# Scaled copies and masks of a delta net moved from VectorE to ScalarE and GpSimd, with new planner figures and a table of chosen moves

## The chip, the cores and the metric

The kernel runs on one core of one Trainium2 chip. A core has five engines, each with its own queue that is worked in order: TensorE (PE, matrix products, results in PSUM), VectorE (DVE), ScalarE (ACT), GpSimd (POOL) and SyncE (SP, which here issues all DMAs). Engines wait for each other through semaphores. The metric is the time on the device in microseconds, lower is better.

## The reference

One step of a two-layer decoder for a prompt of 512 tokens and a sample group of 8 x 8 tokens that share all weights; all arrays are float32, the model width is 1024. Layer 0 mixes tokens by pooling, layer 1 by a gated delta net; each mixer is followed by a SwiGLU block of width 2816, and every block sits between two RMS norms. What the change touches is the delta net, 16 value heads of 128 on 8 key heads of 128. Cut to its core, for one chunk of tokens:

```python
decay = exp(where(causal, gc[i] - gc[j], -inf))       # gc: running sum of the log gates
t_mat = eye + strict(kb @ k.T * decay)                # kb = k * beta
u = solve(t_mat, v * beta); w = solve(t_mat, kb * exp(gc))
qk = q @ k.T * decay
q_dec = q * exp(gc); k_dec = k * exp(gc_last - gc)
# over the chunks, in order:
v_new = u - w @ S
o = q_dec @ S + qk @ v_new
S = S * exp(gc_last) + k_dec.T @ v_new
```

Before it, q, k and v come from one projection of 6176 columns, a causal convolution over four tokens and SiLU, and q and k are normalised by head. After it, o is normalised by head, gated by SiLU(z) and projected back.

## The kernel before

**Tiling and stages.** Activations lie transposed, 128 channels on the partitions by 576 tokens (512 + 64). To keep float32 accuracy at the fast matmul rate every operand is split in a high and a low part: `Weights.split` (line 767) makes `wh` with a copy on ACT and `wl` = raw - wh on DVE, `mm3` (line 775) issues three matmuls for each pair of tiles. The trace shows these stages, in order of time: pooling mixer and its norms, the first SwiGLU block (`ffn`, with `Strassen` for its larger part, to about 440 us), the delta net with its projections (about 500 to 1070 us), the output projection with its norms, the second SwiGLU block, and the last norm.

**The delta net** runs in four groups (`GRP`) of two key heads and four value heads. `project(G)` (line 1316) makes q, k, v of a group: 8 weight tiles of 128 columns, matmuls into the PSUM banks `ps_m`, copies `u` on ACT, the convolution `ac` as three fused instructions on DVE, transposes into `ps_x`, and from there `vt` (prompt) and `vs` (samples), scaled by `nk`, both on DVE. `core(G)` (line 1680) then works in spans of 128 tokens (`SPANS` = 4; the chunk of the reference is 64, the result does not depend on it). It loads the running gate sums as rows, adds the mask `bar` (0 or -1e30) on DVE or POOL, and takes four exponentials on ACT: this is `QD`, the decay. With it `Uw` (the strict part of t_mat) and QD (qk) are made from `ps_k`. `inv32` (line 1209) inverts blocks of 32 on DVE (tiles `ia`, `ii`), a few products put them together. `scan` (line 1611) is the recurrence: for each span and key head `pk` = products with the state S, `rs` (DVE), `t1` = gcq x pk (DVE), `pv` = Uw x rs, `vn` = bet x pv (DVE), `ve` = kde x vn (DVE or POOL), the new state from kt x ve, the output from QD x vn, then scaled by `rq` on DVE. `sample_heads` (line 1541) does the same for the 8 sample sequences, with `ve` split again in `vH` and `vL`. bet, kde, gcq, ngc, rq and nk are small tables with one number for each token and head.

**What sets the order.** No order is written out. Between `plan.start()` and `plan.finish()` the class `Plan` only records the operations with what they read and write. An operation that may run on either of two engines is recorded through `EITHER` (DVE or POOL). `finish` (line 272) then plans the whole kernel as a list: `cost` (line 160) gives each operation a duration by engine, kind and width, `forward` (line 428) puts the ready operation of best rank on each engine, with latencies between engines (`LAT`), a clock model of PE, and idle matmuls (`ps_w`, of `ones`) that it sets into PSUM banks not in use while PE would stand still for long; `backward` finds the latest start of each operation in the plan found, which gives the ranks for the next round. First come 40 rounds with random changes of the ranks, then 16 passes of `refined`: windows of 60 us in steps of 30 us, in each up to 40 random trials, the best one kept. The order so found is issued, so each engine's queue is fixed, and the engines' real semaphores do the rest. All recorded instructions have one line in the profile, L319, the line in `finish` that issues them; they are told apart by the tiles' names (L315 is an idle matmul).

Of the kernel before, what the change touches and what calls it, by code (L numbers as in the profile page):

```python
# [20 lines left out]
P = 128  # L21
# [20 lines left out]
VH = 16  # L42
# [14 lines left out]
class Plan:  # L57
# [8 lines left out]

    LAT = {"PE": 55.0, "ACT": 36.0, "DVE": 36.0, "POOL": 70.0, "SP": 60.0}
# [8 lines left out]
    PASSES, SPAN, STEP, TRIES, FEW = 16, 60000.0, 30000.0, 40, 6  # L76
# [83 lines left out]
    def cost(self, eng, method, out, ins, k):  # L160
# [24 lines left out]
        if eng == "POOL":  # L185
            if method in ("memset", "tensor_copy"):
                t = 0.85 * n + (100 if method == "memset" else 183)
            elif method == "affine_select":
                t = 1.1 * n + 190
            else:  # L190
                bc = any(list(x.ap)[-1][0] == 0 for x in ins if self.size(x) > 1)
                t = (1.75 if bc else 2.2) * n + 180
            return t - 60, t
# [3 lines left out]
        elif method == "scalar_tensor_tensor":  # L197
            t = 1.04 * n + 210
# [8 lines left out]
    def put(self, method, calls, a, k):  # L207
# [39 lines left out]
        if "PE" in calls:  # L247
# [3 lines left out]
            work *= rows * min(1.0, 0.25 * -(-cols // 32)) / 128  # L251
        elif method == "activation":
            mode = self.TABLE.get(str(a[2]).split(".")[-1], 0)
        cost = {e: self.cost(e, method, outs[0], ins, k) for e in calls}
        two = method in ("tensor_tensor", "scalar_tensor_tensor", "tensor_scalar", "tensor_copy") \
            and not any(x.space == PSUM for x in ins)
        self.ops.append((calls, cost, a, k, sorted(preds), mode, work, next(iter(calls)), two, method,
                         {x.tensor.name for x in ins + outs if x.space == PSUM}))
# [13 lines left out]
    def finish(self):  # L272
# [35 lines left out]
        for _ in range(self.PASSES):  # L308
            found = self.refined(best, draw)
            if found[0] < best[0]:  # L310
                best = found
# [9 lines left out]
    def refined(self, plan, draw):  # L321

        late = self.backward(plan[1], plan[2])
        rank = [-t for t in late]
        order = sorted(range(len(late)), key=late.__getitem__)
        names = [self.name(o) for o in self.ops]
        done, state, a, first = ([], []), None, 0.0, 0

        def behind(found, b):

            nonlocal first
            log, times, taken, busy = found[-2], found[-1], found[2], 0.0
            worst = max((t - late[i] for (i, e), (t, _) in zip(log, times) if e is not None), default=-1e12)
            while first < len(order) and state is not None and state[2][order[first]]:
                first += 1
            k = first
            while k < len(order) and taken[order[k]]:
                k += 1
            return worst if k == len(order) else max(worst, b - late[order[k]])

        while True:
            b = a + self.SPAN
            best = None
            tries = self.TRIES
            k = 0
            while k < tries:
                trial = rank
                if k:
                    off, by = {}, draw.choice(self.STIR[2:])
                    trial = rank[:]  # L350
                    for i in window:
                        off.setdefault(names[i], by * (2.0 * draw.random() - 1.0))
                        trial[i] += off[names[i]]
                found = self.forward(trial, state, b, late, best and best[0])
                k += 1
                if found is None:
                    continue
                value = behind(found, b)
                if k == 1:
                    window = [i for i, e in found[-2] if e is not None]  # L360
                    work = sum(self.ops[i][1]["PE"][0] for i, e in found[-2] if e == "PE")
                    if work > 0.995 * self.SPAN:
                        tries = self.FEW
                if best is None or value < best[0]:
                    best = value, trial
            rank = best[1]
            found = self.forward(rank, state, a + self.STEP)
            done[0].extend(found[-2])
            done[1].extend(found[-1])
            state, a = found[:-2], a + self.STEP  # L370
            if not found[0]:
                return max(found[3].values()), *done

# [54 lines left out]
    def forward(self, rank, state=None, until=None, due=None, limit=None):  # L428
# [4 lines left out]
        if state is None:  # L433
# [13 lines left out]
            quiet = {}  # L447
        else:
            todo, left, taken, free, ready, avail, when, mode, dma, port, phases, fast, recent, busy, turn, still, \
                quiet = state  # L450
            left, taken, when, recent = left[:], taken[:], when[:], recent.copy()
            free, mode, port, turn, still, quiet = (dict(v) for v in (free, mode, port, turn, still, quiet))
# [54 lines left out]
        while todo:  # L507
# [40 lines left out]
            if limit is not None and t - due[i] >= limit:  # L548
                return None
            if mine is not q:  # L550
                q.remove((-rank[i], i))
                heapq.heapify(q)
# [7 lines left out]
            if e == "PE":  # L560
                note(t, ops[i][6])
                done += hold * (fast - 1)
                hold *= fast
            taken[i] = True
# [17 lines left out]
            for j in succ[i]:  # L582
                to = ops[j][7]
                at = t + hold if to == e == "PE" else end + self.LAT[to]
# [5 lines left out]
        if until is None:  # L590
            return max(free.values()), order, times
        return (todo, left, taken, free, ready, avail, when, mode, dma, port, phases, fast, recent, busy, turn, still,
                quiet, order, times)

    def take(self, e, q, taken, mode):

        while taken[q[0][1]]:
            heapq.heappop(q)
        best = q[0]
        if self.ops[best[1]][5] not in (0, mode) and self.HOLD.get(e):  # L600
            same = min((x for x in q if not taken[x[1]] and self.ops[x[1]][5] in (0, mode)), default=None)
            if same is not None and same[0] - best[0] < self.HOLD[e]:
                best = same
        q.remove(best)
# [1408 lines left out]
```

## Time and profile before

| | |
|---|---|
| time, median of 3 runs | 1575.35 us (1569.87 to 1575.95) |
| profiled execution, its own time | 1574.86 us |
| its span, first to last instruction | 1573.1 us |
| instructions | 30432 |
| busy: PE, weight loads | 1535.2 us (98%), 1471.2 us (94%) |
| busy: DVE, ACT, POOL | 1192.2 us (76%), 788.5 us (50%), 127.0 us (8%) |
| granted PE clock | 0.996 |
| DMA | 197.86 MB, mean 126 GB/s |

PE's matmuls are pipelined, so that the record of one runs on into the next; a gap shorter than that does not show as idle time. A row of a group of instructions reads: line, engine, operation, what it writes <- what it reads, shape, count, busy time and mean of one in ns, and the idle time of the engine just before them with what ended it. A row of waits reads: who waited <- for whom, us in total, times, the longest.

### The profile page before, as it was taken

The numbers are of one execution on the slowest core, as the hardware profiler recorded it, in microseconds if no ns is written. First come the engines' busy times: TensorE is split into PE (matmuls) and PEld (weight loads), VectorE is DVE, ScalarE is ACT, GpSimd is POOL, SyncE is SP. The second block draws the span as 40 slices with busy tenths as digits, with TensorE's granted clock in tenths as the row PEclk, the third lists the DMA queues.
The fourth block names the chain that finished last, engine by engine and source line by source line (L and its number), as shares of the span: only waits on it lengthen the run. The fifth ranks groups of instructions, "written<-read, shape, count | busy, mean of one in ns | idle before, by whom it ended". The sixth has DMA issues, their size and how long they took to land. (4 is left out here: it accounts for less than half of the span.)

```text
span 1573.1 us, 30432 instructions
## 1 busy us (share of the span) xinstructions
PE 1535.2 (98%) x11931; PEld 1471.2 (94%) x11931; DVE 1192.2 (76%) x2377; ACT 788.5 (50%) x1655; POOL 127.0 (8%) x257
## 2 busy tenths in 40 slices
PE   8999999999999999999999999999999999999997
PEld 8999999999999988898899889899999999999997
DVE  6894566677686898897998899668797485766855
ACT  7663443435556955453563553425465453434553
POOL 4110000000010021100220121000020000000000
PEclk9999999999999999999999999999999999999999
DMA  6464323232566332425243433655864432233253
GB/s 184 134 181 124 103 71 112 61 107 80 168 179 171 110 102 79 141 69 143 83 132 93 126 109 100 204 160 172 244 196 136 144 93 83 76 100 108 76 169 105
DMA packets 344902, 197.86 MB, mean 126 GB/s; under 512 B 13547, under 2 KB 337740, under 8 KB 344751
## 3 DMA queue, kind: packets, MB, share of 16 engines
q1 hardware_dynamic: 344759, 195.92, 43.0%
q8 instruction: 94, 1.54, 0.4%
q14 instruction: 49, 0.40, 0.1%
HBM read 165.60 MB, written 30.52 MB: 125 GB/s over the span
## 5 line engine op out<-in xcount | busy, mean ns | idle before, releaser
L319 ACT ACTIVATE wh<-wraw 128x1024 fp32r<-128x1024 f32 (+4 forms) x240 | 232.7, 975 | 215.0 <-PE ps_A L319 74.3
L319 DVE TENSOR_TENSOR wl<-wraw,wh 128x1024 fp32r<-128x1024 f32 (+4 forms) x232 | 257.3, 1115 | 66.5 <-ACT wh L319 49.4
L319 PE MATMUL ps_m<-hH,wh 128*128 128x256 f32 (+1 forms) x832 | 248.8, 311 | 2.1 <-ACT zz L319 1.5
L319 PE MATMUL ps_m<-hL,wh 128*128 128x256 f32 (+1 forms) x832 | 248.0, 309 | 0.0
L319 PE MATMUL ps_m<-hH,wl 128*128 128x320 f32 (+1 forms) x832 | 243.4, 307 | 0.0
L319 PEld LDWEIGHTS ps_m<-hH,wh 128*128 128x128 f32 x832 | 154.8, 189 | 7.4 <-ACT zz L319 2.7
L319 PEld LDWEIGHTS ps_m<-hL,wh 128*128 128x128 f32 x832 | 155.1, 189 | 3.2 <-issue 1.7
L319 PEld LDWEIGHTS ps_m<-hH,wl 128*128 128x128 f32 x832 | 153.7, 189 | 2.5 <-issue 0.8
L319 PE MATMUL ps_B<-hH,wh 128*128 128x320 f32 (+1 forms) x444 | 129.8, 305 | 0.2 <-DVE yo L319 0.2
L319 PE MATMUL ps_B<-hL,wh 128*128 128x320 f32 (+1 forms) x444 | 128.6, 304 | 0.0
L319 PE MATMUL ps_B<-hH,wl 128*128 128x320 f32 (+1 forms) x444 | 128.6, 304 | 0.0
L319 PE MATMUL ps_A<-hH,wh 128*128 128x256 f32 (+1 forms) x432 | 118.7, 290 | 0.5 <-DVE yo L319 0.5
L319 PE MATMUL ps_A<-hL,wh 128*128 128x256 f32 (+1 forms) x432 | 118.7, 292 | 0.1
L319 PE MATMUL ps_A<-hH,wl 128*128 128x256 f32 (+1 forms) x432 | 118.2, 292 | 0.0
L319 PE MATMUL ps_A<-aH,wh 128*128 128x288 f32 x352 | 99.3, 297 | 1.4 <-ACT wh L319 1.4
L319 PE MATMUL ps_A<-aL,wh 128*128 128x288 f32 x352 | 100.0, 295 | 0.0
L319 PE MATMUL ps_A<-aH,wl 128*128 128x288 f32 x352 | 99.7, 297 | 0.0
L319 PE MATMUL ps_B<-aH,wh 128*128 128x288 f32 x352 | 98.9, 297 | 0.5 <-DVE xa L319 0.5
L319 PE MATMUL ps_B<-aL,wh 128*128 128x288 f32 x352 | 98.6, 297 | 0.0
L319 PE MATMUL ps_B<-aH,wl 128*128 128x288 f32 x352 | 96.6, 296 | 0.0
L319 PEld LDWEIGHTS ps_B<-hH,wh 128*128 128x128 f32 x444 | 82.1, 188 | 1.0 <-issue 0.5
L319 PEld LDWEIGHTS ps_B<-hH,wl 128*128 128x128 f32 x444 | 81.9, 188 | 0.3 <-DVE wl L319 0.2
(467 smaller groups left out, 4063.8 us busy)
## 6 DMA issues: line engine op xcount, KB each, us to landing
wraw<-in_ffn_w_in_dram SPq DMA_DIRECT2D x77, 512.0 KB
wraw<-in_gdn_w_in_dram SPq DMA_DIRECT2D x56, 512.0 KB
graw<-in_ffn_w_in_dram SPq DMA_DIRECT2D x33, 512.0 KB
wraw<-in_ffn_w_out_dram SPq DMA_DIRECT2D x32, 448.0 KB
wraw<-in_gdn_w_out_dram SPq DMA_DIRECT2D x24, 512.0 KB
wraw<-in_ffn_w_out_dram SPq DMA_DIRECT2D x32, 320.0 KB
St<-in_state_gdn_rec_dram SPq DMA_DIRECT2D x32, 256.0 KB
out_dram<-St SPq DMA_DIRECT2D x32, 256.0 KB
```

Of the source, the lines that this page charges most:

```text
L319: calls[e](*a, **k)
```

## The change

- **Planner.** A result that ACT hands to ACT itself arrives 88 ns later (`SAME`). On DVE and ACT an instruction that starts at another base partition than 0, or follows one, starts 32 ns after the end of the one before (`REBASE`, with a new last field in each recorded operation). Three durations change: POOL copies of more than two dimensions, narrow fused instructions on DVE, `tensor_scalar` from PSUM. Durations are rounded to an eighth of a ns. The 16 passes of random trials are replaced by 5 passes over a fixed table, `CHOSEN`: for each window of 30 us a list of seeds, each of which moves the ranks of the window's operations by a hash of the seed and the number of the tile's name (`moved`).
- **Scaled copies.** `vs`, both `t1`, the first span's output `vv`, and `ve` are made by ACT with a scale of one number per partition, one instruction for each 128 columns. `ve` no longer reads vn: it comes straight from PSUM with the scale `bk` = bet x kde, a new small table that DVE fills for each key head. In `sample_heads` `vH` comes straight from PSUM the same way, and `vL` as one fused DVE instruction per 128 columns.
- **Masks.** The 16 additions of `bar` become `affine_select` on POOL that writes -1e30 outside the triangle; `bar` itself is gone.

The diff, without the numbers of the table and without the removed body of `refined`:

```diff
+    SAME = {"ACT": 88.0}
+    REBASE = 32.0
...
-    PASSES, SPAN, STEP, TRIES, FEW = 16, 60000.0, 30000.0, 40, 6
+    SPAN, STEP = 60000.0, 30000.0
+    CHOSEN = (
...
     )
...
         if eng == "POOL":
-            if method in ("memset", "tensor_copy"):
+            if method == "tensor_copy" and len(list(out.ap)) > 2:
+                t = 5.5 * n + 250
+            elif method in ("memset", "tensor_copy"):
                 t = 0.85 * n + (100 if method == "memset" else 183)
             elif method == "affine_select":
...
         elif method == "scalar_tensor_tensor":
-            t = 1.04 * n + 210
+            t = 1.04 * n + (210 if ps or n > 64 else 152)
+        elif method == "tensor_scalar" and ps:
+            t = 1.09 * n + 200
...
-            work *= rows * min(1.0, 0.25 * -(-cols // 32)) / 128
+            work = round(8 * work * rows * min(1.0, 0.25 * -(-cols // 32)) / 128) / 8
...
-        cost = {e: self.cost(e, method, outs[0], ins, k) for e in calls}
+        cost = {e: tuple(round(8 * t) / 8 for t in self.cost(e, method, outs[0], ins, k)) for e in calls}
...
+        base = any(x.space != DRAM and x.offset >= list(x.ap)[0][0] for x in ins + outs)
         self.ops.append((calls, cost, a, k, sorted(preds), mode, work, next(iter(calls)), two, method,
-                         {x.tensor.name for x in ins + outs if x.space == PSUM}))
+                         {x.tensor.name for x in ins + outs if x.space == PSUM}, base))
 
...
-        for _ in range(self.PASSES):
-            found = self.refined(best, draw)
-            if found[0] < best[0]:
-                best = found
+        numbers = {}
+        self.number = [numbers.setdefault(self.name(o), len(numbers)) for o in ops]
+        for chosen in self.CHOSEN:
+            best = self.refined(best, chosen)
...
+    def refined(self, plan, chosen):
+
+        rank = [-t for t in self.backward(plan[1], plan[2])]
+        done, state, a = ([], []), None, 0.0
+        chosen = {int(w): [int(x) for x in seeds.split()] for w, seeds in (p.split(":") for p in chosen.split(";"))}
         while True:
...
+            seeds = chosen.get(round(a / self.STEP), ())
+            if seeds:
+                window = [i for i, e in self.forward(rank, state, a + self.SPAN)[-2] if e is not None]
+                for seed in seeds:
+                    self.moved(rank, window, seed)
+            a += self.STEP
...
+    def moved(self, rank, window, seed):
+
+        by, part, low = (300.0, 1000.0, 3000.0)[seed % 3], (1, 4, 16)[seed // 3 % 3], 0xffffffff
+        off = {}
+        for i in window:
+            k = self.number[i]
+            if k not in off:
+                y = k * 0x9e3779b1 + seed * 0xc2b2ae35 & low
+                y = (y ^ y >> 13) * 0x27d4eb2f & low
+                x = seed * 0x9e3779b1 + k * 0x85ebca6b & low
+                x = (x ^ x >> 15) * 0x2c1b3c6d & low
+                x = (x ^ x >> 12) * 0x297a2d39 & low
+                off[k] = 0.0 if (y ^ y >> 15) % part else by * (2.0 * ((x ^ x >> 15) / 4294967296.0) - 1.0)
+            rank[i] += off[k]
...
+            elif e in past:
+                if past[e][1] or ops[i][11]:
+                    late = max(past[e][0] + self.REBASE - t, 0.0)
+                    hold, done = hold + late, done + late
+                past[e] = t + done, ops[i][11]
...
-                at = t + hold if to == e == "PE" else end + self.LAT[to]
+                at = t + hold if to == e == "PE" else end + self.LAT[to] + (self.SAME.get(e, 0.0) if to == e else 0.0)
...
+    bk = sp.tile([P, SP1, VH], F32, name="bk")
...
-        bar = cst.tile([P, P], F32, name="bar")
-        DVE.tensor_scalar(bar, t_gt, -1e30, None, op0=mult)
...
+                            DVE.tensor_tensor(bk[:, :, h2], bet[:, :, h2], kde[:, :, h2], op=mult)
...
-                    DVE.tensor_scalar(vs[:SMP, i], pv, nk[:SMP, SPANS, kh:kh + 1], None, op0=mult)
+                    ACT.activation(vs[:SMP, i], pv, AF.Copy, scale=nk[:SMP, SPANS, kh:kh + 1])
...
-                rs, t1, vn, ve = sn[lo, 0], sn[up, 1], sn[:, 2], sn[:, 3]
+                rs, t1, vn = sn[lo, 0], sn[up, 1], sn[:, 2]
...
-                DVE.tensor_tensor(t1, pk[up, 0].rearrange("p (e v) -> p e v", e=2),
-                                  gcq[up, SPANS, h2].unsqueeze(2).to_broadcast([SMP, 2, P]), op=mult)
+                for e in range(2):
+                    ACT.activation(t1[:, e], pk[up, 0, e * P:(e + 1) * P], AF.Copy,
+                                   scale=gcq[up, SPANS, 2 * kh + e:2 * kh + e + 1])
...
-                EITHER.tensor_tensor(ve, vn, kde[:, SPANS, h2].unsqueeze(2).to_broadcast([P, 2, P]), op=mult)
                 vH = cp_.tile([P, 2, P], F32R, name="vH", tag="vH", bufs=1)
                 vL = cp_.tile([P, 2, P], F32R, name="vL", tag="vL", bufs=1)
-                split2(ve, vH, vL)
+                for e in range(2):
+                    by = bk[:, SPANS, 2 * kh + e:2 * kh + e + 1]
+                    ve = pv[:, 0, e * P:(e + 1) * P]
+                    ACT.activation(vH[:, e], ve, AF.Copy, scale=by)
+                    DVE.scalar_tensor_tensor(out=vL[:, e], in0=ve, scalar=by, in1=vH[:, e].bitcast(F32),
+                                             op0=mult, op1=sub)
                 yield 0.6
...
-                        DVE.tensor_tensor(t1, pk[:, 1].rearrange("p (e v) -> p e v", e=2),
-                                          gcq[:, s, hh].unsqueeze(2).to_broadcast([P, 2, P]), op=mult)
+                        for e in range(2):
+                            ACT.activation(t1[:, e], pk[:, 1, e * P:(e + 1) * P], AF.Copy,
+                                           scale=gcq[:, s, hh.start + e:hh.start + e + 1])
...
-                    EITHER.tensor_tensor(ve, vn, kde[:, s, hh].unsqueeze(2).to_broadcast([P, 2, P]), op=mult)
+                    for e in range(2):
+                        ACT.activation(ve[:, e], pv[:, 0, e * P:(e + 1) * P], AF.Copy,
+                                       scale=bk[:, s, hh.start + e:hh.start + e + 1])
...
-                        DVE.tensor_scalar(vv, pov, rqc, None, op0=mult)
+                        ACT.activation(vv, pov, AF.Copy, scale=rqc)
...
-                EITHER.tensor_tensor(de, de, bar.unsqueeze(1).to_broadcast([P, 4, P]), op=add)
+                POOL.affine_select(de, de, [[0, 4], [1, P]], ALU.is_ge, -1e30, base=0, channel_multiplier=-1)
```

More of the change, by code (lines that the diff above doesn't have):

```diff
@@ L75 @@
     ROUNDS, STIR, SEED = 40, (0.0, 0.0, 300.0, 1000.0, 3000.0), 2
-    PASSES, SPAN, STEP, TRIES, FEW = 16, 60000.0, 30000.0, 40, 6
+    SPAN, STEP = 60000.0, 30000.0
+    CHOSEN = (
[125 rows of a table added]
+    )
     def __init__(self, tc):
@@ L319, in finish @@
                 calls[e](*a, **k)
[L321 to L339, printed above, removed]
-        while True:
[L342 to L367, printed above, removed]
@@ new lines, in refined @@
+    def refined(self, plan, chosen):
+        rank = [-t for t in self.backward(plan[1], plan[2])]
+        done, state, a = ([], []), None, 0.0
+        chosen = {int(w): [int(x) for x in seeds.split()] for w, seeds in (p.split(":") for p in chosen.split(";"))}
+        while True:
+            seeds = chosen.get(round(a / self.STEP), ())
[4 more added lines that the diff above has]
+            a += self.STEP
+            found = self.forward(rank, state, a)
@@ L368, in refined @@
             done[0].extend(found[-2])
             done[1].extend(found[-1])
-            state, a = found[:-2], a + self.STEP
+            state = found[:-2]
             if not found[0]:
                 return max(found[3].values()), *done
+    def moved(self, rank, window, seed):
[11 more added lines that the diff above has]
+            rank[i] += off[k]
@@ L426, in backward, with forward @@
         return late
-    def forward(self, rank, state=None, until=None, due=None, limit=None):
+    def forward(self, rank, state=None, until=None):
         ops, succ = self.ops, self.succ
@@ L447, in forward @@
             quiet = {}
+            past = {"DVE": (0.0, False), "ACT": (0.0, False)}
         else:
             todo, left, taken, free, ready, avail, when, mode, dma, port, phases, fast, recent, busy, turn, still, \
-                quiet = state
+                quiet, past = state
             left, taken, when, recent = left[:], taken[:], when[:], recent.copy()
-            free, mode, port, turn, still, quiet = (dict(v) for v in (free, mode, port, turn, still, quiet))
+            free, mode, port, turn, still, quiet, past = (dict(v) for v in (free, mode, port, turn, still, quiet, past))
             ready = {e: v[:] for e, v in ready.items()}
@@ L547, in forward @@
             i = self.take(e, mine, taken, mode.get(e))
[L548 to L552, printed above, removed]
+            q.remove((-rank[i], i))
+            heapq.heapify(q)
             hold, done = ops[i][1][e]
@@ L592, in forward @@
         return (todo, left, taken, free, ready, avail, when, mode, dma, port, phases, fast, recent, busy, turn, still,
-                quiet, order, times)
+                quiet, past, order, times)
     def take(self, e, q, taken, mode):
-        while taken[q[0][1]]:
-            heapq.heappop(q)
-        best = q[0]
+        q = [x for x in q if not taken[x[1]]]
+        best = min(q)
         if self.ops[best[1]][5] not in (0, mode) and self.HOLD.get(e):
-            same = min((x for x in q if not taken[x[1]] and self.ops[x[1]][5] in (0, mode)), default=None)
+            same = min((x for x in q if self.ops[x[1]][5] in (0, mode)), default=None)
             if same is not None and same[0] - best[0] < self.HOLD[e]:
                 best = same
-        q.remove(best)
-        heapq.heapify(q)
         return best[1]
@@ L750, in masks @@
         DVE.scalar_tensor_tensor(out=eye2, in0=eyo, scalar=par, in1=eye2, op0=mult, op1=add)
-        return t_gt, bar, s_le2, s_gt2, s_gt_r, s_in, s_st, eye2
+        return t_gt, s_le2, s_gt2, s_gt_r, s_in, s_st, eye2
     def dup(ap):
@@ L1199, in finish0 @@
                 pre_norm(tp, back[0], acc2, hf, G_MPRE + NC)
-            t_gt, bar, s_le2, s_gt2, s_gt_r, s_in, s_st, eye2 = masks(tp)
+            t_gt, s_le2, s_gt2, s_gt_r, s_in, s_st, eye2 = masks(tp)
             s_le = s_le2[:, :SMP]
```

125 rows, old and new, of the table CHOSEN are left out of this document.

## The prediction

> **What bounds the kernel now.** I read the page first, then the busy time of each engine by stage, then who TensorE (PE) waits for in the stage that stands out, then single instructions there.
>
> ```profile
> span 1573.1 us, 30432 instructions
> ```
>
> The busy times by stage; columns: stretch, its length, then PE, weight loads, VectorE (DVE), ScalarE (ACT), GpSimd (POOL), each in us with its instructions, granted clock, DMA.
>
> ```profile
> 0.00:40.00 40.00, 35.21 (x235) 32.78 (x236) 28.07 (x74) 29.29 (x70) 18.05 (x77) 0.91 0.67 181
> 40.00:540.00 500.00, 499.12 (x3717) 490.51 (x3716) 359.97 (x642) 263.32 (x472) 22.20 (x31) 1.00 0.43 125
> 540.00:1000.00 460.00, 441.21 (x3740) 401.28 (x3738) 412.87 (x1001) 230.51 (x639) 72.21 (x134) 1.00 0.38 109
> 1000.00:1100.00 100.00, 98.40 (x795) 91.25 (x796) 68.05 (x135) 40.84 (x110) 1.25 (x1) 1.00 0.59 175
> 1100.00:1540.00 440.00, 435.90 (x3266) 431.80 (x3265) 307.89 (x504) 211.56 (x341) 13.30 (x14) 1.00 0.45 132
> 1540.00:1573.00 33.00, 25.34 (x187) 23.60 (x186) 15.31 (x27) 12.96 (x26) 0.00 (x0) 0.95 0.25 79
> ```
>
> PE is the bound everywhere: it is without work 37.8 us of the span, and half of that, 460 - 441.2 = 18.8 us, lies between 540 and 1000 us, where the four groups of the delta net run. There DVE is busy 412.87 of 460, 89.8%; in the other long stretches it has a quarter free. So DVE is the second bound of this stage and of no other. Part of PE's busy time is filler besides (matmuls of ones that keep the clock up while nothing is ready); the same stretches for the tile ps_w alone:
>
> ```profile
> 40.00:540.00 500.00, 2.03 (x10) 1.65 (x10) 1.00 0.43 125
> 540.00:1000.00 460.00, 5.92 (x40) 5.22 (x40) 1.00 0.38 109
> 1000.00:1100.00 100.00, 1.05 (x8) 0.98 (x8) 1.00 0.59 175
> 1100.00:1540.00 440.00, 2.89 (x20) 2.55 (x20) 1.00 0.45 132
> ```
>
> PE's waits between 540 and 1000 us (us in total, times, longest), the rows in which it waits for DVE:
>
> ```profile
> PE ps_x L319 <- DVE vt L319: 3.0, 4, 1.4
> PE ps_x L319 <- DVE vs L319: 2.4, 4, 0.9
> PE ps_k L319 <- DVE TQ L319: 2.0, 2, 1.1
> PE ps_k L319 <- DVE QD L319: 1.8, 3, 1.0
> PE ps_k L319 <- DVE Uw L319: 1.3, 4, 0.7
> PE ps_k L319 <- DVE T L319: 0.7, 2, 0.4
> ```
>
> They sum to 11.2 us of the 18.8, 60%. One of them, instruction by instruction:
>
> ```profile
> 704.04 0.31 PE L319 MATMUL ps_m<-hH,wh 128*128 128x320 f32 x1
> 704.19 0.31 PE L319 MATMUL ps_m<-hL,wh 128*128 128x320 f32 x1
> 704.45 0.31 PE L319 MATMUL ps_m<-hH,wl 128*128 128x320 f32 x1
> 705.09 0.34 DVE L319 TENSOR_SCALAR vs<-ps_x,nk 64x128 f32<-64x128 f32 x1
> 705.57 0.41 PE L319 MATMUL ps_x<-ident,ac 128*128 128x128 f32 x2 [0.81 <-DVE vs L319]
> ```
>
> Undisturbed, matmuls of this width start 0.15 apart (704.04, 704.19). From 704.45 to 705.57 it is 1.12: 0.97 is lost, while 0.81 is shown as idle, because a matmul's record runs on past the start of its successor. About 0.16 us is thus hidden in each stall. What PE waits for is a bank that the DVE copy vs has to empty.
>
> **The change part by part.** It has two halves: what the engines must do, and the order. PE's real matmuls, the DMAs and SP's queue keep their number.
>
> *Off DVE, onto ACT and POOL.* The operations that go, and below them the nearest rows for what comes:
>
> ```profile
> L319 DVE TENSOR_TENSOR QD<-QD,bar 128x512 f32<-128x512 f32 x16 | 10.9, 682 | 2.3 <-DMA QD<-gc_d 2.3
> L319 DVE TENSOR_SCALAR vs<-ps_x,nk 64x128 f32<-64x128 f32 x16 | 5.4, 338 | 0.2
> L319 DVE TENSOR_TENSOR t<-ps_k,gcq 128x256 f32<-128x256 f32 x24 | 9.9, 414 | 0.0
> L319 DVE TENSOR_TENSOR ve<-vn,kde 128x256 f32<-128x256 f32 x28 | 11.5, 419 | 0.2
> L319 DVE TENSOR_SCALAR vt<-ps_s,rq 128x256 f32<-128x256 f32 x8 | 3.7, 478 | 4.0 <-PE ps_s L319 4.0
> L319 DVE TENSOR_TENSOR sn<-ps_k,gcq 64x256 f32<-64x256 f32 x8 | 3.4, 428 | 0.2
> L319 DVE TENSOR_TENSOR sn<-sn,kde 128x256 f32<-128x256 f32 x6 | 2.9, 485 | 0.0
> L319 DVE TENSOR_TENSOR vL<-sn,vH 128x256 fp32r<-128x256 f32 x6 | 2.5, 422 | 0.9 <-ACT vH L319 0.9
> ...
> L319 DVE SCALAR_TENSOR_TENSOR Uw<-ps_k,bet,QD 128x128 f32<-128x128 f32 x64 | 18.9, 342 | 1.3 <-PE ps_k L319 1.1 <-issue 0.2
> L319 ACT ACTIVATE S<-ps_s 128x128 f32<-128x128 f32 x16 | 3.5, 273 | 7.0 <-PE ps_s L319 7.0
> L319 ACT ACTIVATE u<-ps_m 128x256 f32<-128x256 f32 x56 | 20.9, 378 | 25.0 <-PE ps_m L319 23.5 <-PE ps_x L319 1.2
> L319 ACT ACTIVATE y<-ps_A,prm 128x256 f32<-128x256 f32 x8 | 3.6, 470 | 0.7 <-PE ps_A L319 0.7
> L319 POOL TENSOR_SCALAR_AFFINE_SELECT eyo<-eyo 128x512 f32<-128x512 f32 x1 | 0.9, 869 | 0.1
> L319 POOL COPY u<-cstt 128x24 f32<-128x24 f32 x18 | 8.9, 503 | 26.6 <-ACT u L319 9.6 <-issue 7.9 <-ACT cstt L319 6.2
> ```
>
> DVE loses 10.9 + 5.4 + 9.9 + 11.5 + 3.7 + 3.4 + 2.9 + 2.5 = 50.2 us. It gains 16 fused instructions that make vL from PSUM, 16 x 0.342 = 5.5, and eight tiny products for bk, at most 8 x 0.342 = 2.7 and by their 10 columns nearer half, 1.3. Not all lies in the tight stage, as the instructions on ve between 540 and 1000 us show:
>
> ```profile
> 540.00:1000.00 460.00, 14.23 (x48) 7.79 (x48) 8.12 (x20) 4.00 (x4) 1.00 0.38 109
> ```
>
> 24 of 32 (4 of them on POOL): the last of four groups scans after 1000 us. So three quarters of the last six removed rows count, 25.4 of 33.9; of the masks, four a group with the first group's ahead of the stage, 8.2; all of vs, which belongs to the projections, 5.4. In the stage that is 39.0 off and 0.75 x 5.5 + 1.3 = 5.4 on. The planner now gives a POOL copy of three dimensions 5.5 ns an element instead of 0.85, so some of these go to DVE: between none and 18 at the 0.338 of the wider vs copy, 6.1; I take 4, the upper half, since the trace has them dear on POOL (503 ns). Net in the stage: 30 us, DVE from 412.9 to 383.
>
> ACT gets 160 scaled copies of 128 columns: 16 vs, 16 t1 and 16 vH of the samples, 48 t1 and 64 ve of the scan. The plain copy of that width takes 273 ns; a per-partition scale adds 470 - 378 = 92; 365 each, 58.4, and eight of 256 columns at 470, 3.8: 62.2 in all, less the eight vH copies it did before. In the stage some 46, so ACT goes from 230.5 to 277 of 460. That lies in ACT's free time; without it the price is that of the third rival. POOL gets 16 masks of 0.87, 13.9 us, in the stage 10.4 on 72.2, less the few kde products it did. Each mask stands ahead of four exponentials on ACT, at the least the 273 of a plain copy each, 1.1 us, so POOL at 0.87 keeps in front; if it didn't, those exponentials would be late next.
>
> A rule that speaks against the masks stands in the Trainium skill, "SBUF — State Buffer", section "SBUF: two separate sides": VectorE with two SBUF inputs and GpSimd take one shared port pair by an exclusive lock, the later one blocked for the whole instruction. A row with two SBUF inputs (ns min/median/max):
>
> ```profile
> L319 DVE SCALAR_TENSOR_TENSOR ac<-u,cwt,ac x96: 825/836/1452, 513.6 to 977.6; 128x600 f32<-128x600 f32 x96
> ```
>
> The longest took 616 ns more than the median and the median 11 more than the shortest, so in this row blocking is the exception. If by that rule every mask blocked VectorE, 10.4 of the 30 us would be given back, the stage's gain below would fall from 18 to 12, and the time would be 1557.
>
> *What PE gets of it.* The stage offers idle 18.8, filler 5.9, and hidden tails: 19 waits in the rows above at 0.16 are 3.0, and as many again for those of other engines would be 6; I take 5.3. Together 30. The lower end is none of it; the upper end comes from the other side: with DVE at 383 and the same 89.8% of the stage, the stage is 426 long, 34 less. I take the part in which DVE was the releaser, 60%: **18 us**.
>
> *The order.* The planner's new figures (an ACT result read by ACT 88 ns later, 32 ns where the base partition differs, dearer POOL copies) and a table of 5 passes of chosen moves replace a search inside the kernel. No row prices this. Outside the stage and between 40 and 1540 us PE has idle 0.9 + 1.6 + 4.1 and filler 2.0 + 1.1 + 2.9, together 12.5; a better order could take all, a worse one lose as much. I take half as gain, **6 us**, since one figure moves towards the trace: for the POOL copy of 24 columns and 503 ns the old one gives 0.85 x 24 + 183 = 203, the new 5.5 x 24 + 250 = 382. The 4.8 idle of the first 40 us and the 7.7 of the last 33 are chains that the change leaves alone.
>
> Sum: 1574.86 (the profiled execution; 1.8 of it outside the span) - 18 - 6 = 1550.9. The median of the runs is 0.5 higher; I say **1551**.
>
> **The rivals.**
> *DVE was worth more.* The stage shrinks with DVE (34) and most of the 12.5 outside goes (8): 1574.9 - 42 = 1533. For it: an engine at 89.8% that works in a fixed order is late for much that shows as no idle time of PE, in gaps under 0.16 us. Against: only 30 us of loss can be seen.
> *PE doesn't care.* The freed time is hidden behind matmuls anyway, the waits move to ACT: 1570 to 1577, say 1573. For it: no wait in the rows above is over 1.4 us. Against: the 704 us rows, where the moved copy itself held PE.
> *ACT in the recurrence (slower).* ve, vH and t1 now queue on ACT in order, behind the weight copies.
>
> ```profile
> L319 ACT ACTIVATE wh<-wraw 128x1024 fp32r<-128x1024 f32 x159 | 167.5, 1057 | 115.6 <-PE ps_m L319 53.2 <-PE ps_A L319 24.5 <-PE ps_B L319 24.5
> ```
>
> Before, a step had vn then ve on DVE, 0.42 + 0.42; now two copies of 0.365 straight from PSUM, 0.73, plus up to 1.06 behind a weight copy: +0.95. There are 16 serial steps and 8 sample heads: 24 x 0.95 = 23; at ACT's 60% busy, 14 us: 1589 if nothing is gained elsewhere. Behind them on ACT stand the next wh copies, and for those wait wl on DVE and the projection's matmuls. It decides once ACT is so full that the plan can't set the scaled copies ahead of wh; against it, ACT sat idle 115.6 us ahead of its wh copies. The Trainium skill, "ScalarE: Activation LUTs", section "Rules for kernel authors", says the same in general: multiplications belong on VectorE, not ScalarE. The rows agree per element (365 ns for 128 columns against 414 for 256), and 62 us of ACT for 50 of DVE is the price of its breach.
> *The table doesn't fit.* Its numbers mean something only for the list of operations they were chosen on. If it was another list, ranks are moved at random by up to 3 us, and each of the 23 slices of the stage may look like the worst one:
>
> ```profile
> 980.00:1000.00 20.00, 17.51 (x228) 16.19 (x226) 16.95 (x35) 10.54 (x23) 3.29 (x4) 1.00 0.57 175
> ```
>
> 23 x 2.49 = 57 idle instead of 18.8, +38, against the 24 gained: 1589. Against it: the table is densest in its windows 15 to 35 of 30 us, 450 to 1080, where the trace has the delta net.
>
> **How the numbers follow.** Forecast 0.50, more from DVE 0.24, no effect 0.13, ACT in the recurrence 0.08, table unfit 0.05. A measurement tells 0.5%, 8 us, from no change: the first two are faster (0.74), the third is the same (0.13), the last two slower (0.13). The range leaves out the slower cases and the far end of the second: 1530 (all 12.5 outside and the 34: 1528) to 1576; the forecast's own is 1541 (34 gained) to 1562 (12).
>
> **What would show it.** Right: between 540 us and the end of the third group's projection PE idle falls from 18.8 to under 10, DVE busy by about 30 (over the span by 50.2 - 6.8 - 4 = 39), ACT's rises by some 60 over the span, the wait of ps_x for DVE vs is gone, and the stages before and after keep their lengths. Wrong: DVE falls and PE's idle time stays (second rival), PE waits for ACT ve or vH (third), or PE idles and filler grows in the weight-streaming stages too (fourth). A gain that lies outside 540 to 1100 us would be the order's, not the engines'.

## The result, and the profile after

The changed kernel takes 1553.05 us (median of 4 runs, 1552.07 to 1555.61) against 1573.22 us (4 runs, 1569.87 to 1575.95): 0.9875 of the time before, interval 0.9848 to 0.9902. The forecast was 1551. The number holds; the runs below show that its reason does not.

The head of the page after:

```profile
span 1550.3 us, 30447 instructions
...
PE 1519.0 (98%) x11875; PEld 1456.1 (94%) x11875; DVE 1162.7 (75%) x2292; ACT 831.7 (54%) x1809; POOL 130.1 (8%) x261
```

DVE lost 29.5 us, ACT took on 43.2, POOL 3.1. The busy times by stage after (stretch, its length, then PE, weight loads, DVE, ACT, POOL with their instructions, clock, DMA):

```profile
40.00:540.00 500.00, 497.98 (x3730) 489.28 (x3730) 365.19 (x664) 267.14 (x485) 23.55 (x38) 1.00 0.44 125
540.00:1000.00 460.00, 447.29 (x3875) 409.43 (x3877) 393.19 (x925) 269.36 (x777) 78.38 (x135) 1.00 0.42 118
1000.00:1100.00 100.00, 96.86 (x748) 89.44 (x739) 66.71 (x125) 48.05 (x129) 0.24 (x1) 1.00 0.63 181
1100.00:1540.00 440.00, 438.11 (x3293) 434.19 (x3292) 307.33 (x507) 215.89 (x349) 11.16 (x12) 1.00 0.43 124
```

The filler (tile ps_w) after, in the same stretches:

```profile
40.00:540.00 500.00, 1.95 (x10) 1.53 (x10) 1.00 0.44 125
540.00:1000.00 460.00, 0.39 (x2) 0.30 (x2) 1.00 0.42 118
1000.00:1100.00 100.00, 0.00 (x0) 0.00 (x0) 1.00 0.63 181
1100.00:1540.00 440.00, 2.28 (x16) 2.02 (x16) 1.00 0.43 124
```

In the stage PE idle fell from 18.8 to 12.7 us and filler from 5.9 to 0.4. Over the span there are 11817 real matmuls in both kernels (all of PE's less the filler's 114 before, 58 after), so the 22.8 us of span split into three: idle 37.9 to 31.3, filler 18.6 to 10.6, and the records of the real matmuls 1516.6 to 1508.4. The last part, 8.2 us, is at least in part time that stalls hide behind a record's tail; the granted clock can have a share, since it was 0.91 in the first 40 us before and 1.00 there after, which is up to 3.6 us.

Who PE waits for after, between 540 and 1000 us:

```profile
PE ps_x L453 <- DVE vt L453: 3.8, 4, 1.8
PE ps_k L453 <- DVE QD L453: 1.4, 2, 0.9
PE ps_s L453 <- DVE sn L453: 1.2, 4, 0.4
PE ps_s L453 <- DVE vs L453: 1.2, 3, 0.6
PE ps_s L453 <- ACT ve L453: 1.0, 4, 0.3
PE ps_x L453 <- ACT qk L453: 0.7, 1, 0.7
PE ps_x L453 <- ACT vs L453: 0.7, 2, 0.5
```

The wait of ps_x for the copy vs went from 2.4 us to 0.7, now on ACT (the row of ps_s for DVE vs is another use of that tile); the largest, for vt, an operation that the change leaves alone, did not shrink (3.0 to 3.8). The moved operations in the list of groups after, with two that follow them on DVE:

```profile
L453 ACT ACTIVATE ve<-ps_s,bk 128x128 f32<-128x128 f32 x64 | 21.1, 366 | 16.8 <-DVE vn L453 10.0 <-PE ps_s L453 6.5
L453 ACT ACTIVATE t<-ps_k,gcq 128x128 f32<-128x128 f32 x48 | 16.3, 367 | 20.2 <-PE ps_k L453 10.2 <-DVE rs L453 5.4 <-DVE vt L453 4.3
L453 DVE SCALAR_TENSOR_TENSOR rs<-ps_k,ngc,vt 128x128 f32<-128x128 f32 x48 | 15.6, 346 | 10.1 <-ACT t L453 8.9 <-PE ps_k L453 1.1
L453 POOL TENSOR_SCALAR_AFFINE_SELECT QD<-QD 128x512 f32<-128x512 f32 x16 | 14.1, 900 | 30.1 <-DMA QD<-gc_d 18.5 <-PE ps_s L453 11.4
L453 DVE TENSOR_TENSOR vn<-ps_s,bet 128x256 f32<-128x256 f32 x32 | 13.3, 422 | 9.5 <-ACT ve L453 7.2 <-PE ps_s L453 2.0
```

The copies cost what was forecast (366 ns for 365), the masks a little more (900 for 869). New is that DVE waits on ACT: rs for t 8.9 us, vn for ve 7.2 us. DVE's idle time ahead of these two groups grew little, though, from 8.0 to 10.1 and from 7.8 to 9.5 us; before, nearly all of it was ended by PE.

Where in time did the gain come? By the rows of the stages, idle time and filler together fell from 24.7 to 13.1 us between 540 and 1000 us and from 7.0 to 4.2 between 1100 and 1540; between 40 and 540 us they rose from 2.9 to 4.0. What PE has begun by a given moment says the same. From the start to 540 and to 1000 us, first everything, then the filler, before:

```profile
0.00:540.00 540.00, 534.34 (x3950) 523.29 (x3951) 388.04 (x714) 292.61 (x541) 40.24 (x108) 0.99 0.45 129
0.00:1000.00 1000.00, 975.55 (x7688) 924.57 (x7688) 800.90 (x1713) 523.12 (x1179) 112.45 (x242) 0.99 0.42 120
0.00:540.00 540.00, 8.73 (x46) 7.52 (x46) 0.99 0.45 129
0.00:1000.00 1000.00, 14.65 (x86) 12.75 (x86) 0.99 0.42 120
```

and after:

```profile
0.00:540.00 540.00, 533.26 (x3960) 521.39 (x3961) 391.16 (x730) 295.94 (x552) 40.30 (x113) 1.00 0.46 129
0.00:1000.00 1000.00, 980.54 (x7833) 930.82 (x7837) 784.35 (x1654) 565.30 (x1328) 118.68 (x248) 1.00 0.44 124
0.00:540.00 540.00, 7.96 (x40) 6.73 (x40) 1.00 0.46 129
0.00:1000.00 1000.00, 8.35 (x42) 7.03 (x42) 1.00 0.44 124
```

Less the filler that is 3904 real matmuls by 540 us before and 3920 after, 16 more, some 2 us at the 0.14 us that one took on average until then. By 1000 us it is 7602 before and 7791 after, 189 more. So most of the gain lies in the stage, as the prediction had it.

The transposes that begin the inverse of the first and of the fourth group (count, ns min/median/max, first and last start), before:

```profile
L319 DVE STREAM_TRANSPOSE ia<-Uw x2: 2042/2059/2076, 556.5 to 558.6; 32x1024 f32<-32x1024 f32 x2
L319 DVE STREAM_TRANSPOSE ia<-Uw x4: 2000/2022/2048, 941.1 to 947.7; 32x1024 f32<-32x1024 f32 x4
```

and after:

```profile
L453 DVE STREAM_TRANSPOSE ia<-Uw x2: 2023/2032/2041, 547.3 to 549.3; 32x1024 f32<-32x1024 f32 x2
L453 DVE STREAM_TRANSPOSE ia<-Uw x4: 2025/2026/2058, 924.7 to 930.9; 32x1024 f32<-32x1024 f32 x4
```

The first group's inverse starts 9.2 us earlier, the fourth's 16.4. The first of these is mostly a new place in the order and not time won, since PE is some 2 us ahead there. By the prediction's own test, a gain outside 540 to 1100 us would be the order's; this one lies inside for the most part. But the test cannot tell the two causes apart: e_old_ops_own_table below moves no operation and has begun 3905 real matmuls by 540 us and 7760 by 1000 us, so the order alone gains in the same place.

### The profile page after: what moved, and what is told of

It reads as the page before. It is cut to its first block, busy times and chain, and to the rows that moved or that the text cites. A ratio compares the mean times of both kernels' runs of the same rounds, so it can differ in the third digit from the quotient of the medians.

```text
span 1550.3 us, 30447 instructions
## 1 busy us (share of the span) xinstructions
PE 1519.0 (98%) x11875; PEld 1456.1 (94%) x11875; DVE 1162.7 (75%) x2292; ACT 831.7 (54%) x1809; POOL 130.1 (8%) x261
## 4 chain that ended last, share of the span: by engine, by line
PE 81%; DVE 9%; ACT 4%; DMA 4%; issue 2%; POOL 0%; DVEq 0%; SPq 0%; ACTq 0%
PE ps_B L453 27%; PE ps_A L453 24%; PE ps_m L453 17%; PE ps_s L453 4%; PE ps_k L453 4%; PE ps_x L453 2%; DVE wl L453 2%; PE ps_e L453 1%; PE ps_n L453 1%; DVE ac L453 1%; ACT wh L453 1%; DMA wraw<-in_ffn_w_out_dram 1%; DVE Uw L453 1%; DMA wraw<-in_gdn_w_out_dram 1%; DMA wraw<-in_ffn_w_in_dram 1%
## 5 line engine op out<-in xcount | busy, mean ns | idle before, releaser
L453 PE MATMUL ps_m<-hH,wh 128*128 128x320 f32 (+1 forms) x832 | 250.7, 311 | 0.0
L453 PE MATMUL ps_m<-hL,wh 128*128 128x320 f32 (+1 forms) x832 | 248.5, 307 | 0.0
L453 PE MATMUL ps_B<-aH,wl 128*128 128x288 f32 x352 | 100.1, 297 | 0.2
L453 DVE SCALAR_TENSOR_TENSOR ac<-u,cwt,ac 128x600 f32<-128x600 f32 x96 | 81.9, 857 | 3.8 <-ACT ac L453 3.3
```

What stands on the lines that cost most here:

```text
L453: calls[e](*a, **k)
```

## The experiments

Three theories. **A**, the prediction's: the relief of DVE gives most of the gain (18 of 24 us). **B**: the order gives it, through the planner's figures or through the table of chosen moves; where an expectation says B1 and B2, they differ in whether the figures are worth nothing or something once a table is there. **C**: plans made in the same way lie some us apart, and part of the gain is a lucky draw. **A2** in some expectations is the weaker form of A: a good order needs the relieved DVE. All ratios are to the kernel before, run beside (1574.66, 1575.78 and 1574.83 us in the three groups of runs).

### Each half alone

**e_ops_only.** The kernel before with its planner, figures and random search; only the operations move, by the change's own lines:

```diff
-                    DVE.tensor_scalar(vs[:SMP, i], pv, nk[:SMP, SPANS, kh:kh + 1], None, op0=mult)
+                    ACT.activation(vs[:SMP, i], pv, AF.Copy, scale=nk[:SMP, SPANS, kh:kh + 1])
...
-                EITHER.tensor_tensor(de, de, bar.unsqueeze(1).to_broadcast([P, 4, P]), op=add)
+                POOL.affine_select(de, de, [[0, 4], [1, P]], ALU.is_ge, -1e30, base=0, channel_multiplier=-1)
```

> The kernel before with only the operations moved (scaled copies and vH, vL, bk on ScalarE, masks on GpSimd); the planner, its figures and its search are those of before. Theory A (the relief of VectorE is worth 18 of the 20 us found): about 1555, filler and idle time of PE fall in the delta net. Theory B (the relief alone is worth little, the order found by the table carries it): 1566 or more. Theory C (a plan is a draw, any new search gives another time): anything within the spread that the other seed shows.

Measured: 1580.49 us, 1.0035 [1.0018, 1.0052]. Theory A falls in its plain form. The stretch of the delta net, before:

```profile
520.00:1080.00 560.00, 540.13 (x4525) 492.10 (x4524) 481.34 (x1148) 278.23 (x788) 74.90 (x140) 1.00 0.42 120
```

and with the operations moved alone, by stretch and by PE's waits there:

```profile
520.00:1080.00 560.00, 531.35 (x4444) 480.59 (x4443) 457.24 (x1059) 325.44 (x944) 68.20 (x143) 0.99 0.41 116
```

```profile
PE ps_x L319 <- DVE vt L319: 9.0, 7, 2.6
PE ps_s L319 <- ACT ve L319: 3.7, 12, 0.5
PE ps_k L319 <- DVE QD L319: 3.6, 6, 1.0
```

DVE is 24.1 us lighter in this stretch (22.5 over the whole span), and PE stands idle 28.7 us where it stood 19.9 (48.4 and 37.9 over the span). DVE's own vt now comes late for 9.0 us, and 12 small waits for ACT's ve are new.

**e_figures_only.** The reverse: old operations and old random search, only `SAME`, `REBASE` and the cost lines new.

```diff
+    SAME = {"ACT": 88.0}
+    REBASE = 32.0
...
+            if method == "tensor_copy" and len(list(out.ap)) > 2:
+                t = 5.5 * n + 250
```

> The kernel before with only the planner's new figures (88 ns from ScalarE to itself, 32 ns after another base partition, dearer GpSimd copies, two other durations); operations and random search of before. Theory A: half of the order's 6 us, 1570. Theory B: some 10 us, 1563 or less. Theory C: within the spread of the other seed.

Measured: 1564.49 us, 0.9939 [0.9918, 0.996], near theory B's 1563 and not A's 1570.

**e_ops_figures_search.** Both of the edits above together, still with the old random search in place of the table.

> The changed kernel with the random search of before in place of the table: moved operations and new figures. Theory A: 1573 - 18 - 3 = 1552, the table adds no more than 3. Theory B: over 1563, the table is what matters. Theory C: as the first run, give or take the spread.

Measured: 1567.43 us, 0.9947 [0.9926, 0.9967]. Theory A had 1552; the operations add nothing to the figures.

**e_before_seed3.** The kernel before with another random start of its search:

```diff
-    ROUNDS, STIR, SEED = 40, (0.0, 0.0, 300.0, 1000.0, 3000.0), 2
+    ROUNDS, STIR, SEED = 40, (0.0, 0.0, 300.0, 1000.0, 3000.0), 3
```

> The kernel before with another seed of its random search (3 for 2), nothing else. It measures how far two plans of equal making lie apart. Theories A and B: within 4 us of 1573. Theory C: 8 us or more from it.

Measured: 1567.2 us, 0.9947 [0.9929, 0.9965]. A new draw alone, with nothing else changed, brought 7.5 us, close to the 8 that theory C asked for and outside the 4 of the others. So theory C counts: the four plans of this group lie between 1564 and 1580, and neither the loss of the moved operations (5.8 us) nor the gain of the figures (10.2 us) stands clear of what one draw can do.

### The table with and without the moved operations

To compare lists of operations fairly, each needs a table chosen for it. New tables were made in one way: over the same windows, moves with random seeds were kept if they lowered the planner's own lateness.

**e_old_ops_own_table.** The changed kernel with all moved operations put back on DVE (the diff of e_ops_only read backwards, with `bk` gone and `bar` back) and a table of its own.

> The changed planner, but all operations back on VectorE as before, with a table of moves found for that list of operations (six passes, some 500 trials a window). Theory B (the order made the time): 1554, as the change, give or take 5. Theory A2 (a good order needs the relieved VectorE): 1561 or more, since the same care can then not reach the change's time.

Measured: 1544.57 us, 0.9802 [0.9769, 0.9835]. That is still faster than theory B's 1554 give or take 5, and far from A2's 1561 or more.

**e_new_ops_own_table.** The changed kernel with nothing but another table (six passes for five), made with the same effort:

```diff
     CHOSEN = (
-        "0: 29557 68768 61061 95313 13858 31142 6088 54786 97423 54486 74385 53842 60713 26823 86926 59342 13774 "
...
+        "0: 58915 85405 27519 63944 91204 94573 85137 49965 95138 3806 99738 4525 62944 54304 92148 66640 "
...
```

> The changed kernel with another table, found in the same way and with the same effort as that of the run with the old operations. Theories A2 and B: as the change, 1548 to 1556; the distance to the run with the old operations is what the moved operations are worth under equal care: 0 to 5 for B, 8 or more for A2.

Measured: 1544.15 us, 0.9797 [0.9777, 0.9816]. It beats both kernels, and the 1548 to 1556 expected; its table has about twice the moves of the change's (4295 against 1989, that of the run above 4491). Beside the run above it is the clearest of the study: with equal care for the order, the moved operations make no difference that can be measured. The stretch of the delta net with the old operations and their own table, the filler in it, and PE's waits:

```profile
520.00:1080.00 560.00, 550.40 (x4637) 508.93 (x4636) 486.06 (x1152) 297.63 (x817) 91.37 (x164) 0.99 0.45 127
```

```profile
520.00:1080.00 560.00, 2.70 (x16) 2.28 (x16) 0.99 0.45 127
```

```profile
PE ps_x L610 <- DVE vt L610: 3.1, 2, 1.8
PE ps_k L610 <- DVE QD L610: 1.3, 2, 0.9
PE ps_x L610 <- DVE ii L610: 1.2, 2, 0.8
```

DVE is busier than before the change (486.1 against 481.3 us of 560), yet PE's idle time is halved, 9.6 against 19.9, and its filler went from 6.6 to 2.7. The waits for vs, TQ and Uw that the prediction counted against DVE's load are no longer among the largest, with these operations still on DVE. (This profile is of the longest of the four runs, 1549.55 us, with the lowest granted clock, 0.987; the shortest took 1539.1 at 0.996. Its real matmuls took 1511.6 us over the span against 1506.4 with the second table below, whose profile has a clock of 0.993; longer records can hide idle time, so the half may flatter. That second profile has 11.3 us idle in this stretch, and 6.6 of filler.)

**e_empty_table.** The changed kernel with its five passes, none of which moves anything:

```diff
-        for chosen in self.CHOSEN:
+        for chosen in ["0: "] * len(self.CHOSEN):
```

> The changed kernel with no moves in its five passes: each pass only plans again from the latest starts of the one before. Theory B: 1566 to 1580, about where the random search left the same operations, or above. Theory A2: 1560 or less, since the relief is still there.

Measured: 1591.42 us, 1.0106 [1.0075, 1.0137]. Theory B had 1566 to 1580 or above, A2 1560 or less. Without the choices the change is slower than the kernel before. Against the kernel before, the change gains 20 us, this kernel loses 15.6, the old random search with the same operations and figures gains 7.2. So the choices are worth some 35 us against none and some 12 against the old search.

**e_other_table.** The same table with every seed raised by 9, which keeps each move's size and its share of the operations, but hits others:

```diff
-        chosen = {int(w): [int(x) for x in seeds.split()] for w, seeds in (p.split(":") for p in chosen.split(";"))}
+        chosen = {int(w): [int(x) + 9 for x in seeds.split()] for w, seeds in (p.split(":") for p in chosen.split(";"))}
```

> The changed kernel with 9 added to every seed of the table: each move keeps its size and its share of the names, but moves others. That is a table which does not fit the list. Theory B and the fourth rival of the prediction: 1588 or more, idle and filler time of TensorE up by 38 or more in the delta net. Theory A2: below 1575.

Measured: 1621.96 us, 1.0291 [1.0268, 1.0313]. The filler in the stretch of the delta net:

```profile
520.00:1080.00 560.00, 27.35 (x190) 25.20 (x190) 0.99 0.39 111
```

6.6 us before, 27.4 here: the planner itself sees that PE would stand and fills in. An order that does not fit costs 46 us against before and some 66 against the change. Theory B had 1588 or more. That is how far the order alone can move this kernel.

### What the figures are worth, and how far tables lie apart

**e_old_figures_own_table.** As e_old_ops_own_table, with the old figures too, and its own table:

```diff
-    SAME = {"ACT": 88.0}
-    REBASE = 32.0
+    SAME = {}
+    REBASE = 0.0
...
-            if method == "tensor_copy" and len(list(out.ap)) > 2:
-                t = 5.5 * n + 250
```

> Operations and duration figures of before, but with the changed way of ordering (five or more passes over a table found for this list, six here). Theory B1 (the table carries the gain, the figures little): 1544 to 1550, as the other lists with a table of their own. Theory B2 (a careful order pays only where the figures are true): 1556 or more.

Measured: 1555.3 us, 0.9877 [0.9855, 0.99]: 19.5 us from the new way of ordering, with neither the moved operations nor the new figures (but for the rounding of durations), as much as the whole change gives, though by a table with about twice its moves. It lies between B1's 1544 to 1550 and B2's 1556 or more, nearer to B2.

**e_old_ops_table_2.** e_old_ops_own_table with a table from another random start.

> As the run with the old operations and their own table, but the table comes from another random start; by the planner's own count its order is 6.5 us longer than the first one's. It shows how far two tables for one list lie apart: 1544 to 1552 where that count means something, equal to the first (1545) where it doesn't.

Measured: 1549.74 us, 0.9845 [0.983, 0.986], some 5 us behind the first table, about what the planner's count (6.5) had. With a table the new figures are thus worth 5.6 us in this group of runs and 10.7 by the other table; since two tables of one kernel differ by 5 us, that is likely but not settled.

**e_new_ops_long_2** and **e_new_ops_long_3.** e_new_ops_own_table with two more tables, each from a longer search (seven passes, three times the trials) and another random start.

> The changed kernel with a table from three times the trials and another random start; the planner counts 1.5 us less than for the first own table. 1540 to 1545 if more care still pays; 1544 to 1548 if it is used up.

> The same with a third random start; the planner's count is the first own table's. Together with the others it shows the spread among tables made alike: within 4 us of each other, all under the change's 1553.

Measured: 1547.13 us, 0.9823 [0.9809, 0.9838], and 1551.73 us, 0.9854 [0.9839, 0.9868]. More trials did not help, and these two and the first own table lie up to 7.6 us apart where 4 were expected. The orders that were chosen with care, side by side (idle is the span less PE's busy time, real the records of the 11817 matmuls that are no filler, DVE its busy time over the span; all in us):

| kernel | ratio | span | PE idle | filler | real | DVE |
|---|---|---|---|---|---|---|
| before (random search) | 1 | 1573.1 | 37.9 | 18.6 | 1516.6 | 1192.2 |
| e_ops_only (random search) | 1.0035 | 1577.0 | 48.4 | 16.4 | 1512.2 | 1169.7 |
| old operations, own table | 0.9802 | 1547.8 | 24.2 | 12.0 | 1511.6 | 1177.6 |
| old operations, table 2 | 0.9845 | 1550.9 | 29.2 | 15.3 | 1506.4 | 1188.4 |
| old operations, old figures, table | 0.9877 | 1552.3 | 35.0 | 11.2 | 1506.1 | 1190.8 |
| the change | 0.9875 | 1550.3 | 31.3 | 10.6 | 1508.4 | 1162.7 |
| moved operations, own table | 0.9797 | 1542.9 | 28.7 | 10.7 | 1503.5 | 1162.6 |
| moved operations, long 2 | 0.9823 | 1545.5 | 31.2 | 10.0 | 1504.3 | 1164.1 |
| moved operations, long 3 | 0.9854 | 1549.7 | 32.6 | 10.0 | 1507.1 | 1162.6 |

The last column does not follow the ratio. The means of the two with old operations and new figures and of the three with moved operations and tables other than the change's are 0.9824 and 0.9825, though two of these three had the longer search. The granted clock of these profiles lies between 0.987 (old operations, own table) and 0.997 (the change), and in that one kernel the time went from 1539.1 us at 0.996 to 1549.55 at 0.987, so that a few us between two single rows say little.

## Why the prediction was right, and where its reason was wrong

**PE bounds the kernel; 30 us can be had in the stage, 12.5 outside.** Right as a size: the best orders took 25 to 30 us from the span. The tails were counted only inside the stage; over the span the records of the real matmuls shrank by 8.2 us, of which the rows do not say where.

**DVE is the second bound of the stage, so its relief pays.** This step failed. 89.8% busy was read as a limit. The old operations with their own table run at 486 of 560 us of DVE with half the idle time (11.3 us and not 9.6 with the second table); the moved operations with the old planner run at 457 with more. The waits "for DVE" were real, but those for vs, TQ and Uw all but went with another order alone, so they came from an instruction's place in DVE's queue more than from want of time on DVE. A share of waits by releaser says who was late, not that a lighter engine would have been in time.

**The term of 18 us (60% of 30).** It measured about zero: 5.8 us lost with the old figures and search, 2.9 lost with the new figures (1564.49 to 1567.43), nothing with tables. The runs do not exclude some 5 us either way.

**The order, 6 us.** This is the term that carries the result, and it was sized at half of what lay outside the stage since "no row prices this". It is worth some 20: 10.2 came with the figures alone (one draw moved 7.5), and the table is worth some 12 in place of the search. The old figures with a table gave 19.5, so a table can bring it nearly alone. The forecast of 1551 came out because about as much loss was there as the two terms took together, and the order recovered it, not the relief of DVE. With one term at about zero and the other at three times its size, that the sum came out some 2 us from the measured time is luck.

**The counts and prices.** The 50.2 us that were to leave DVE have left, and the prices were right (365 and 470 ns forecast, 366 and 472 measured on ACT; 342 and 341 for vL); only the masks were dearer, 900 ns for 869. DVE's busy time fell by 29.5 where 39 was forecast; added over the listed groups its records fell by 36, and busy time counts overlapping records once. ACT rose by 43.2, not 60: count times mean of the new copies is 62.2 as forecast, but as busy time, overlaps counted once, they are 57.2; less the 3.3 of the old vH that is 53.9, and six fewer table loads took 7.7 off again.

**The rivals.** "PE doesn't care" was right about the operations and wrong about the time, since it gave the order nothing. "ACT in the recurrence" shows as a trace: 12 waits for ve, 3.7 us, in e_ops_only, and DVE's 16 us of waits on ACT after the change, most of which stand where it waited for PE before; a price of 14 us was not seen. "The table doesn't fit" did not happen to this change, but its mechanism is real and was priced too low: it forecast 14 us over before and the run measured 46, and some 66 over the table that fits. The Trainium skill, "ScalarE: Activation LUTs", section "Rules for kernel authors", would keep the multiplications on VectorE; e_ops_only agrees in sign with its 0.35%, which is less than one draw can do, and the runs with tables show neither gain nor harm.

**What would show it.** The signs came in part: the wait for vs shrank to 0.7, DVE's busy time fell by 19.7 us between 540 and 1000 us where about 30 were expected, ACT's rose by 43.2 over the span and not 60, and PE idle in the stretch stayed at 12.7 instead of under 10. Before the stage PE gained some 2 us only. The last sign, a gain that lies outside, could not have told the order from the engines, since the order gains inside the stage as well; only the runs that change one of the two could.

What stays open: which single changes of place in the queues bring the 20 us. The tables move many operations at once, and no run took one move alone.

## What to carry to other kernels

Where each engine works its queue in a fixed order, an engine that is 90% busy and is named in most waits need not be the bound: first give the same work another order, and see whether the waits go. When a change brings new work and a new plan together, give the old work a plan made with the same care, and measure the spread of plans made alike (here 5 to 8 us), before the gain is put down to the work.

## What the hardware showed beside this

The prediction weighed a rule of the Trainium skill ("SBUF — State Buffer", section "SBUF: two separate sides"), by which VectorE with two SBUF inputs and GpSimd lock each other out. Single places after the change fit it. The longest ac, which as a rule takes 0.84 us:

```profile
921.77 2.41 POOL L453 TENSOR_TENSOR wl<-wraw,wh 128x1024 fp32r<-128x1024 f32 x1 [1.54 <-ACT wh L453]
...
922.37 2.46 DVE L453 SCALAR_TENSOR_TENSOR ac<-u,cwt,ac 128x600 f32<-128x600 f32 x1
```

ac started 0.60 us after GpSimd's wl and ended 0.65 us after wl did (924.83 against 924.18): it took 1.62 us more than its usual 0.84, most of the 1.81 us for which wl still ran. The masks that were feared for it show the other side (ns min/median/max):

```profile
L453 POOL TENSOR_SCALAR_AFFINE_SELECT QD<-QD x16: 629/724/1602, 526.5 to 913.0; 128x512 f32<-128x512 f32 x16
```

Here it is the mask that is held up, up to 1602 ns where the shortest took 629. The longest is the first of three in a row that began just after a wl on DVE:

```profile
656.94 1.21 DVE L453 TENSOR_TENSOR wl<-wraw,wh 128x1024 fp32r<-128x1024 f32 x1
657.04 2.78 POOL L453 TENSOR_SCALAR_AFFINE_SELECT QD<-QD 128x512 f32<-128x512 f32 x3 [0.65 <-DMA QD<-gc_d]
```

Over all 16 masks that is 14.1 - 16 x 0.629 = 4.0 us, on an engine that is 8% busy. ac kept its median (836 to 839 ns). The 10.4 us that the rule would have taken from DVE do not show in this row.
